# The normalised chunks of three norms: from three engines to VectorE alone, with the row of scales read in PSUM

## The chip, the cores and the metric

The kernel runs on one core of one Trainium2 chip. The metric is device time in microseconds (us). The engines of a core are named as in the profile: PE is TensorE (with PEld, its weight loads), DVE is VectorE, ACT is ScalarE, POOL is GpSimd and SP is SyncE, which here only issues DMAs.

## The reference, cut to what matters

Two transformer layers and one further block work on one sequence of 256 tokens and 1024 channels, all in float32. Each sub-layer begins with the same norm:

```
y = x * rsqrt(mean(x * x, over channels) + 1e-6) * g
h = y * (1 + scale) + shift            # layers 0 and 1; the last block has g alone
out = h @ W                            # the sub-layer's first projection
```

`scale` and `shift` come from a conditioning vector. Sub-layers: a linear recurrence, a routed feed-forward ("PEER": per token and head the 16 best of 128 x 128 experts, then all experts as two dense products with sparse weights), attention with forget gates, a second PEER, and then a block of three mixers and a gated feed-forward.

## The kernel before

**Layout.** Activations lie transposed: 8 chunks of 128 channels (partitions) by 256 tokens. The residual `x` is 8 chunks in SBUF. Every product is made three times in a reduced format (`mm3`): each operand is split in a high part and a low rest, so `out = wh*xh + wh*xl + wl*xh`. For an activation the parts are `hh` and `hl`; for a weight unit of 128 x 1024 they are `whi` and `wlo`.

**The weight stream.** All weights pass through one stream of units (class `Stream`): SP loads a unit (`raw`), ACT or DVE makes `whi`, DVE or POOL makes `wlo`. Which engine does it is fixed when the program is built, by a running estimate of each engine's load (`either`, `soonest`, class `Clock`). Four split units and three raw ones can be ahead of PE.

**The norm, twice.** A norm needs the sums of squares over all channels before it can scale, and PE would wait for that. So `early` starts the next projection on unnormalised input: `before_norm` splits `x*g` into `hh` and `hl`, PE multiplies four weight units (five in the last block) with them, and the per-token scale is applied to the product afterwards. Meanwhile the sums become `rstd` (a power on POOL), and PE spreads `rstd` over all partitions into a row of scales in PSUM: two products with the identity, written to columns 0 to 255 of `r`, a `ps2` tile of two banks (the name `ps<-ident,rstd` in the profile). ACT copies that row to SBUF as `rb`.

**After the early projections**, `after_early` (three of the five norms: the PEER of layer 0, the attention, the PEER of layer 1) does two things. It scales the four early products, `out(i)`: DVE multiplies the product in PSUM with `rb`, copies one column of it, and ACT adds that column as a bias. And it makes the true normalised chunks: chunk by chunk `x*gs*rb`, then `hh` on ACT and `hl` on DVE (`normed_split`). Of the eight chunks in the order `BANKS`, those at even places are made by DVE in one operation (`scalar_tensor_tensor`: x times a column times `rb`), those at odd places by ACT (x times the column, ahead of time) and POOL (times `rb`). PE needs `hh` and `hl`, in that order of chunks, for the next unit's product. In the last block the two norms don't come here: they use `rb` alone (`scaled`, and `unit` of the feed-forward).

**What orders the work.** A scheduler with its own timeline puts the instructions of each engine in an order when the program is built; each engine then runs its own list strictly in that order and waits on semaphores. The three places are called here the first (at about 198 us, PEER of layer 0), the second (1058 us, attention) and the third (1239 us, PEER of layer 1). In the PEERs `W` is scratch memory (the chunks and the queries lie there); at the second place the chunks lie in `raw_qk`. After `out(i)` the PEER multiplies the queries with the keys (`q_scores`, in the profile `pb<-W`), and that needs a PSUM bank which an early product held until `out(i)` had read it.

Of the kernel before, what the change touches and what calls it, by code (L numbers as in the profile page):

```python
# [11 lines left out]
AF = mybir.ActivationFunctionType  # L12
ALU = mybir.AluOpType
# [3 lines left out]
T = 256  # L17
# [299 lines left out]
class Kern:  # L317
# [100 lines left out]
    def early(self, x, gs, shift=None, how=None, count=4):  # L418


        nc, tc, hx, lx = self.nc, self.tc, self.hx, self.lx
        n = T
        if shift is not None:
            n = T + 2
            two = shift[:, 0:NCH, None].to_broadcast([P, NCH, 2])
            nc.scalar.copy(hx[:, :, T:], two)
            nc.vector.tensor_sub(lx[:, :, T:], two, hx[:, :, T:].bitcast(F32))
        outs = [self.ps() for _ in range(4)]
        outs += [o[:, T:] for o in outs[:count - 4]]
        r, b = self.ps2(), None  # L430
        w, step = {}, 0
        groups, rows_at, bcast_at = how or HOW
        groups += tuple((i,) for i in range(4, count))
        for g in groups:
            for i in g:
                w[i] = self.ws.get(i > 3)
            for k, c in enumerate(self.BANKS):
                s = slice(c * P, (c + 1) * P)
                for i in g:
                    with tc.issue_after(b.ins) if b is not None else nullcontext():  # L440
                        mm = self.mm3(outs[i][:, 0:n], *(t[:, s] for t in w[i]), hx[:, c, 0:n], lx[:, c, 0:n],
                                      k == 0, k == NCH - 1)
                    step += 1
                    if step == rows_at:
                        with tc.issue_after(mm.ins):
                            self.pow = r1 = self.rstd_rows(r[:, 512:])
                        for lo in los[1:2]:
                            with tc.issue_after(r1.ins):
                                lo(nc.gpsimd)
                        for lo in los[2:]:  # L450
                            lo(nc.vector)
                    if step == bcast_at:
                        with tc.issue_after(mm.ins):
                            b = self.rstd_bcast(r)
                        nc.scalar.copy(self.rb, r[:, 0:T])
            if g is groups[0]:
                with tc.issue_after(self.last_sq.ins):
                    los = self.ws.begin()
                for lo in los[:1]:
                    lo(nc.vector)  # L460
        self.normed = x, gs, shift
        return outs

    def scaled(self, outs, dst):
# [6 lines left out]
    def after_early(self, outs, dst, slots):  # L471

        nc = self.nc
        x, gs, shift = self.normed
        s = slots[0][:, 0:4]

        def out(i):
            nc.vector.tensor_mul(dst[i], outs[i][:, 0:T], self.rb)
            if shift is not None:
                nc.vector.tensor_copy(s[:, i:i + 1], outs[i][:, T:T + 1])  # L480
                nc.scalar.activation(dst[i], dst[i], AF.Identity, bias=s[:, i:i + 1])

        t = slots[1:]
        for c in self.BANKS[1::2]:
            nc.scalar.activation(t[c], x[:, c], AF.Copy, scale=gs[:, c:c + 1])
        few = len(outs) == 4
        for i in range(2 if few else 0):
            out(i)
        for k, c in enumerate(self.BANKS):
            if k % 2:  # L490
                h = nc.gpsimd.tensor_mul(t[c], t[c], self.rb)
            else:
                nc.vector.scalar_tensor_tensor(t[c], x[:, c], gs[:, c:c + 1], self.rb, op0=ALU.mult, op1=ALU.mult)
        for c in self.BANKS:
            h2 = self.normed_split(t[c], c, shift)
        self.h_there = h.ins, h2.ins
        for i in range(2 if few else 0, len(outs)):
            out(i)
        self.clock.level()
# [1489 lines left out]
```

## Time and profile before

| | us |
|---|---|
| median of 3 runs (2552.61, 2553.39, 2561.49) | 2553.39 |
| the profiled execution's own time | 2553.62 |
| its span | 2551.9 |
| PE busy in the span | 2455.8 (96%) |
| DVE busy | 1715.5 (67%) |
| ACT busy | 1249.5 (49%) |
| POOL busy | 1055.4 (41%) |

Between the span and the execution's own time lie 1.7 us. A timeline row reads: start, duration, engine, line, operation, out<-in with the names of the program, shape, how many instructions are merged in the row, and in brackets how long the engine was idle before it and who ended that. All work is recorded by one helper, so every row has line L225, and rows are told apart by tile names. PEclk is the TensorE clock that was granted, 1.00 for full speed. A row of the stage table gives, for a stretch of the span, the busy time of each engine, and PEclk.

### The profile page before, as it was taken

Reading aid. Unit: us, or ns where it says so; the run is one execution under the profiler, and the core shown is the slowest. Engines: PE = TensorE matmul, PEld = TensorE weight load, DVE = VectorE, ACT = ScalarE, POOL = GpSimd, SP = SyncE. Lnnn points to the kernel's source line nnn. Section 1 sums busy time; section 2 is a strip of 40 time slices with the busy share of each in tenths; the row PEclk is TensorE's granted clock in tenths of the full one; section 3 lists DMA queues with packets and bytes.
Section 4 is the critical chain, followed back from the end, with each engine's and each line's share of the span. In section 5 each row is a group of like instructions: output and inputs, shape, how many; then the busy total and the mean of one; then the engine's idle time right before and its main releaser. Section 6 shows DMA issues by size and latency. Waiting matters only on the chain.

```text
span 2551.9 us, 48864 instructions
## 1 busy us (share of the span) xinstructions
PE 2455.8 (96%) x19264; PEld 2390.3 (94%) x19264; DVE 1715.5 (67%) x3404; ACT 1249.5 (49%) x2031; POOL 1055.4 (41%) x654
## 2 busy tenths in 40 slices
PE   7879999999999999999999999999999999999998
PEld 7879999999999999878899999899999997999996
DVE  8798785765787755673787668465555558557764
ACT  4745555554444444544555555444444444444543
POOL 4477766779522100331577677870000015303310
PEclk9989999999999999998999999999999999999999
DMA  7855566678888865452556566885555554364654
GB/s 274 305 157 182 182 195 192 213 232 293 285 310 312 305 200 184 145 158 66 167 168 199 190 210 215 266 285 185 182 182 184 185 183 132 116 198 153 196 182 139
DMA packets 164134, 517.40 MB, mean 203 GB/s; under 512 B 18224, under 2 KB 51136, under 8 KB 162880
## 3 DMA queue, kind: packets, MB, share of 16 engines
q1 hardware_dynamic: 144720, 463.53, 55.7%
q0 software_dynamic: 8064, 29.36, 3.5%
q10 hardware_dynamic: 11120, 21.38, 2.4%
q8 instruction: 151, 2.47, 0.4%
q14 instruction: 79, 0.65, 0.1%
HBM read 484.85 MB, written 29.36 MB: 202 GB/s over the span
## 4 chain that ended last, share of the span: by engine, by line
PE 73%; DVE 8%; POOL 7%; issue 6%; DMA 4%; ACT 2%; SPq 0%; POOLq 0%; ACTq 0%; DVEq 0%
PE pb L225 38%; PE ps L225 35%; POOL W L225 5%; DVE mraw L225 2%; DVE wlo L225 1%; POOL wlo L225 1%; DVE hl L225 1%; DMA raw<-pv 1%; ACT whi L225 1%; DMA x<-gdram 1%; DVE W L225 0%; DVE tt L225 0%; DVE ri L225 0%; DMA mraw<-mod_ffn 0%; DMA raw<-pu 0%
## 5 line engine op out<-in xcount | busy, mean ns | idle before, releaser
L225 ACT CAST whi<-raw 128x1024 fp32r<-128x1024 f32 x741 | 777.1, 1050 | 945.9 <-PE ps L225 356.4
L225 DVE TENSOR_TENSOR wlo<-raw,whi 128x1024 fp32r<-128x1024 f32 x475 | 622.2, 1311 | 456.2 <-ACT whi L225 449.8
L225 POOL TENSOR_TENSOR wlo<-raw,whi 128x1024 fp32r<-128x1024 f32 x282 | 682.5, 2423 | 454.2 <-ACT whi L225 400.0
L225 PE MATMUL ps<-hh,whi 128*128 128x256 f32 x2736 | 780.6, 285 | 11.8 <-DVE W L225 5.5
L225 PE MATMUL ps<-hl,whi 128*128 128x256 f32 x2736 | 782.4, 286 | 6.7 <-DVE hl L225 6.7
L225 PE MATMUL ps<-hh,wlo 128*128 128x256 f32 x2736 | 777.9, 285 | 8.1 <-DVE wlo L225 5.0
L225 PE MATMUL pb<-hh,whi 128*128 128x256 f32 (+1 forms) x2512 | 715.4, 287 | 11.0 <-ACT whi L225 8.5
L225 PE MATMUL pb<-hl,whi 128*128 128x256 f32 (+1 forms) x2512 | 713.8, 285 | 3.6 <-DVE hl L225 3.4
L225 PE MATMUL pb<-hh,wlo 128*128 128x256 f32 (+1 forms) x2512 | 710.0, 284 | 4.3 <-POOL wlo L225 2.5
L225 PEld LDWEIGHTS ps<-hh,whi 128*128 128x128 f32 x2736 | 524.3, 192 | 13.5 <-DVE W L225 6.2
L225 PEld LDWEIGHTS ps<-hh,wlo 128*128 128x128 f32 x2736 | 525.2, 192 | 10.9 <-DVE wlo L225 6.9
L225 PEld LDWEIGHTS ps<-hl,whi 128*128 128x128 f32 x2736 | 522.6, 191 | 9.6 <-DVE hl L225 7.8
L225 PEld LDWEIGHTS pb<-hh,whi 128*128 128x128 f32 x2512 | 478.1, 191 | 12.8 <-ACT whi L225 9.5
L225 PEld LDWEIGHTS pb<-hh,wlo 128*128 128x128 f32 x2512 | 478.4, 191 | 6.0 <-POOL wlo L225 3.3
L225 PEld LDWEIGHTS pb<-hl,whi 128*128 128x128 f32 x2512 | 478.6, 191 | 4.5 <-DVE hl L225 4.5
L225 POOL TENSOR_TENSOR W<-W 128x256 f32<-128x256 f32 x12 | 9.3, 774 | 527.7 <-ACT W L225 527.7
L225 DVE SCALAR_TENSOR_TENSOR o<-pb,x 128x128 f32<-128x128 f32 (+1 forms) x512 | 196.4, 411 | 28.6 <-PE ps L225 27.5
L225 POOL TENSOR_TENSOR W<-W,x 128x384 f32<-128x384 f32 x128 | 180.1, 1446 | 4.4 <-DMA x<-gdram 2.7
L225 DVE TENSOR_TENSOR o<-pb,x 128x256 f32<-128x256 f32 (+1 forms) x256 | 106.8, 417 | 104.1 <-PE ps L225 72.8
L225 PE MATMUL ps<-o 128*128 128x128 f32 (+1 forms) x768 | 125.9, 276 | 0.0
L225 PEld LDWEIGHTS ps<-o 128*128 128x128 f32 x768 | 105.6, 190 | 0.0
L225 ACT COPY x<-ps 128x384 f32<-128x384 f32 x128 | 61.1, 477 | 55.4 <-PE ps L225 55.2
(400 smaller groups left out, 2891.4 us busy)
## 6 DMA issues: line engine op xcount, KB each, us to landing
raw<-pu SPq DMA_DIRECT2D x256, 512.0 KB, 3.8
raw<-pv SPq DMA_DIRECT2D x256, 512.0 KB, 4.3
x<-gdram SPq DMA_DIRECT2D x128, 192.0 KB, 4.0
raw<-w_rest SPq DMA_DIRECT2D x40, 512.0 KB, 3.8
raw<-pq SPq DMA_DIRECT2D x32, 512.0 KB, 4.0
mraw<-mod_mix SPq DMA_DIRECT2D x24, 512.0 KB, 6.0
gdram<-x ACTq DMA_DIRECT2D x64, 192.0 KB, 2.1
gdram<-x SPq DMA_DIRECT2D x64, 192.0 KB, 2.3
```

The lines of the kernel that those rows point to most:

```text
L225: return f(*args, **kw)
```

## The change

ACT no longer makes the four products x times column ahead of time, POOL no longer multiplies, and the copy of the row of scales to SBUF moves from ACT to DVE. DVE makes all eight chunks and reads the row of scales from `r` in PSUM; `rb` is still used for the early products. The copy moves at all five norms, the chunks at the three with `after_early`.

```diff
@@ in early
-                        nc.scalar.copy(self.rb, r[:, 0:T])
+                        nc.vector.tensor_copy(self.rb, r[:, 0:T])
...
-        self.normed = x, gs, shift
+        self.normed = x, gs, shift, r[:, 0:T]
@@ in after_early
-        x, gs, shift = self.normed
+        x, gs, shift, rp = self.normed
...
         t = slots[1:]
-        for c in self.BANKS[1::2]:
-            nc.scalar.activation(t[c], x[:, c], AF.Copy, scale=gs[:, c:c + 1])
         few = len(outs) == 4
         for i in range(2 if few else 0):
             out(i)
-        for k, c in enumerate(self.BANKS):
-            if k % 2:
-                h = nc.gpsimd.tensor_mul(t[c], t[c], self.rb)
-            else:
-                nc.vector.scalar_tensor_tensor(t[c], x[:, c], gs[:, c:c + 1], self.rb, op0=ALU.mult, op1=ALU.mult)
+        for c in self.BANKS:
+            h = nc.vector.scalar_tensor_tensor(t[c], x[:, c], gs[:, c:c + 1], rp, op0=ALU.mult, op1=ALU.mult)
         for c in self.BANKS:
             h2 = self.normed_split(t[c], c, shift)
```

The scheduler's order differs near the three places, by a single instruction at the copies in the last two norms, and in seven matmul rows ahead of the last norm; elsewhere each engine's list is the same, and every `whi` and `wlo` stays on its engine. Three pieces follow. Tiles are numbered in the order in which they are made, so the same tile has another number before and now.

DVE at the second place, from the first use of the row of scales; `raw_qk<-x,mod_mix` is a chunk, `z` and `og` are the scaled early products, `ps` is the row in PSUM. Before:

```order
L225 TENSOR_TENSOR z<-pb_12279,rb 128x256
L225 COPY raw_qk<-pb_12279 128x1
L225 TENSOR_TENSOR og<-pb_12280,rb 128x256
L225 COPY raw_qk<-pb_12280 128x1
L225 SCALAR_TENSOR_TENSOR raw_qk<-x,mod_mix,rb 128x256 x4
L225 TENSOR_TENSOR og<-pb_12281,rb 128x256
L225 COPY raw_qk<-pb_12281 128x1
L225 CAST whi<-raw 128x1024
L225 SCALAR_TENSOR_TENSOR hl<-raw_qk,mod_mix,hh 128x256 x2
L225 TENSOR_TENSOR og<-pb_12282,rb 128x256
```

Now:

```order
L225 COPY rb<-ps_12279 128x256
L225 SCALAR_TENSOR_TENSOR raw_qk<-x,mod_mix,ps_12279 128x256 x7
L225 TENSOR_TENSOR z<-pb_12275,rb 128x256
L225 COPY raw_qk<-pb_12275 128x1
L225 TENSOR_TENSOR og<-pb_12276,rb 128x256
L225 COPY raw_qk<-pb_12276 128x1
L225 SCALAR_TENSOR_TENSOR raw_qk<-x,mod_mix,ps_12279 128x256
L225 TENSOR_TENSOR og<-pb_12277,rb 128x256
L225 COPY raw_qk<-pb_12277 128x1
L225 CAST whi<-raw 128x1024
L225 SCALAR_TENSOR_TENSOR hl<-raw_qk,mod_mix,hh 128x256 x5
L225 TENSOR_TENSOR og<-pb_12278,rb 128x256
```

The copy and seven chunks now stand ahead of the first early product, and ahead of the first `hl` stand the same operations as before and, in addition, the copy and the four chunks that POOL made. The same holds at the first and the third place.

POOL at the second place; the first `wlo` is of a unit that the early projections use. Before:

```order
L225 TENSOR_TENSOR wlo_12312<-raw_12157,whi_12311 128x1024
L225 TENSOR_TENSOR raw_qk_12413<-raw_qk_12413,rb_101 128x256 x4
L225 TENSOR_TENSOR wlo_12498<-raw_12495,whi_12497 128x1024
L225 TENSOR_TENSOR wlo_12508<-raw_12501,whi_12507 128x1024
L225 TENSOR_TENSOR wlo_12564<-raw_12511,whi_12563 128x1024
```

Now:

```order
L225 TENSOR_TENSOR wlo_12308<-raw_12153,whi_12307 128x1024
L225 TENSOR_TENSOR wlo_12490<-raw_12487,whi_12489 128x1024
L225 TENSOR_TENSOR wlo_12500<-raw_12493,whi_12499 128x1024
L225 TENSOR_TENSOR wlo_12556<-raw_12503,whi_12555 128x1024
L225 TENSOR_TENSOR wlo_12615<-raw_12559,whi_12614 128x1024
```

The four products between the splits of two weight units are gone, so the second split no longer stands behind them. At the third place four products likewise stood behind `wlo_14092` and ahead of `wlo_14102` (now `wlo_14080` and `wlo_14090`).

PE at the third place, right after the early projections; `pb<-W` are the scores of the first three queries, `whi_13934` (now `whi_13926`) is the unit of the first projection on the true chunks. Before:

```order
L225 MATMUL pb3_14075<-W_14025 128x128 x2
L225 MATMUL pb0_14080<-W_14025 128x128 x2
L225 MATMUL pb1_14085<-W_14025 128x128 x2
L225 MATMUL pb3_14090<-hh_104,whi_13934 128x256
L225 MATMUL pb3_14090<-hl_105,whi_13934 128x256
L225 MATMUL pb3_14090<-hh_104,wlo_13935 128x256
```

Now, with the projection's next twelve matmuls left out:

```order
L225 MATMUL pb3_14063<-W_14017 128x128 x2
L225 MATMUL pb0_14068<-W_14017 128x128 x2
L225 MATMUL pb3_14078<-hh_104,whi_13926 128x256
...
L225 MATMUL pb1_14073<-W_14017 128x128 x2
L225 MATMUL pb3_14078<-hl_105,whi_13926 128x256
L225 MATMUL pb3_14078<-hh_104,wlo_13927 128x256
```

The third pair of scores, whose bank the last early product holds, moved from ahead of the projection to behind its thirteenth matmul.

## The prediction

> **What bounds the kernel now.** I read the page's header first, then the busy time by stage, cut at the three places of the change.
>
> ```profile
> span 2551.9 us, 48864 instructions
> core 0: us, PE busy (x) PEld busy (x) DVE busy (x) ACT busy (x) POOL busy (x), PEclk, DMA share, GB/s
> 199.00:215.00 16.00, 11.79 (x90) 10.79 (x89) 16.00 (x44) 8.79 (x23) 12.02 (x8) 1.00 0.50 186
> 215.00:571.00 356.00, 356.00 (x3009) 355.85 (x3009) 256.96 (x905) 193.66 (x377) 257.90 (x110) 1.00 0.64 202
> 1058.00:1076.00 18.00, 13.20 (x77) 11.70 (x77) 15.01 (x30) 10.35 (x23) 10.88 (x7) 0.81 0.50 161
> 1239.00:1258.00 19.00, 13.11 (x84) 12.39 (x83) 18.24 (x46) 8.29 (x22) 10.72 (x8) 0.73 0.41 148
> 1258.00:1604.00 346.00, 346.00 (x2925) 345.84 (x2924) 254.36 (x900) 189.10 (x369) 248.12 (x104) 1.00 0.62 196
> ```
>
> After the first and the third place PE is busy all the time for some 350 us, so a microsecond that PE gains at a place moves everything behind it. At the places themselves PE idles 16.00 - 11.79 = 4.2, 18.00 - 13.20 = 4.8 and 19.00 - 13.11 = 5.9 us: 14.9 us is the whole idle time that the change can reach. DVE is the busiest there. Which wait ends last is read from PE's timeline at the three places:
>
> ```profile
> 208.00 0.39 PE L225 MATMUL pb<-hl,whi 128*128 128x256 f32 x1 [1.44 <-DVE hl L225]
> 210.50 0.38 PE L225 MATMUL pb<-hl,whi 128*128 128x256 f32 x1 [1.33 <-DVE hl L225]
> ...
> 1066.72 0.58 PE L225 MATMUL ps<-hl,whi 128*128 128x256 f32 x1 [3.32 <-DVE hl L225]
> 1069.22 0.58 PE L225 MATMUL ps<-hl,whi 128*128 128x256 f32 x1 [1.48 <-DVE hl L225]
> ...
> 1245.90 0.84 PE L225 MATMUL pb<-W 128*128 128x128 f32 x4 [2.11 <-DVE pb L225]
> 1249.88 1.19 PE L225 MATMUL pb<-W 128*128 128x128 f32 x4 [3.14 <-DVE W L225]
> 1252.56 0.58 PE L225 MATMUL pb<-hl,whi 128*128 128x256 f32 x1 [0.63 <-DVE hl L225]
> ```
>
> Every long wait ends with DVE: an `hl`, or at the third place the early product whose bank the scores need. Why DVE is late stands in its timeline and POOL's at the same places (first, second, third):
>
> ```profile
> 205.43 2.52 DVE L225 SCALAR_TENSOR_TENSOR hl<-W,mod_ffn,hh 128x256 fp32r<-128x256 f32 x1
> 208.26 3.37 DVE L225 SCALAR_TENSOR_TENSOR hl<-W,mod_ffn,hh 128x256 fp32r<-128x256 f32 x4
> 205.12 5.04 POOL L225 TENSOR_TENSOR wlo<-raw,whi 128x1024 fp32r<-128x1024 f32 x2 [1.48 <-DVE whi L225]
> ...
> 1064.10 5.07 DVE L225 SCALAR_TENSOR_TENSOR hl<-raw_qk,mod_mix,hh 128x256 fp32r<-128x256 f32 x2
> 1069.48 2.06 DVE L225 SCALAR_TENSOR_TENSOR hl<-raw_qk,mod_mix,hh 128x256 fp32r<-128x256 f32 x5
> 1060.06 3.56 POOL L225 TENSOR_TENSOR raw_qk<-raw_qk,rb 128x256 f32<-128x256 f32 x4
> 1063.59 5.29 POOL L225 TENSOR_TENSOR wlo<-raw,whi 128x1024 fp32r<-128x1024 f32 x2
> ...
> 1245.76 2.98 DVE L225 SCALAR_TENSOR_TENSOR hl<-W,mod_ffn,hh 128x256 fp32r<-128x256 f32 x2
> 1249.66 3.64 DVE L225 SCALAR_TENSOR_TENSOR hl<-W,mod_ffn,hh 128x256 fp32r<-128x256 f32 x4
> 1245.71 2.35 POOL L225 TENSOR_TENSOR wlo<-raw,whi 128x1024 fp32r<-128x1024 f32 x1
> 1249.47 2.35 POOL L225 TENSOR_TENSOR wlo<-raw,whi 128x1024 fp32r<-128x1024 f32 x1 [1.41 <-issue]
> ```
>
> Five `hl` in a row take 2.06 us, 0.41 each, when POOL is idle. While POOL runs a `wlo`, one `hl` waits for that `wlo` to end: two of them take 5.07 us behind two `wlo` of 5.29. So a `wlo` that falls among the `hl` costs DVE about 2.1 us (5.07 less 2 x 0.41, halved), and PE behind it. There are two such `wlo` at each place.
>
> **The change part by part.** *The chunks.* What they cost now, and what a like operation costs that has one input in PSUM:
>
> ```profile
> L225 DVE SCALAR_TENSOR_TENSOR W<-x,mod_ffn,rb x8: 942/960/2105, 199.4 to 1244.2; 128x256 f32<-128x256 f32 x8
> L225 DVE TENSOR_TENSOR W<-pb,rb x8: 408/411/425, 198.6 to 1249.3; 128x256 f32<-128x256 f32 x8
> L225 ACT COPY rb<-ps x5: 347/373/373, 198.1 to 2361.0; 128x256 f32<-128x256 f32 x5
> 199.39 3.66 DVE L225 SCALAR_TENSOR_TENSOR W<-x,mod_ffn,rb 128x256 f32<-128x256 f32 x4
> 1059.75 3.28 DVE L225 SCALAR_TENSOR_TENSOR raw_qk<-x,mod_mix,rb 128x256 f32<-128x256 f32 x4
> 1240.44 4.72 DVE L225 SCALAR_TENSOR_TENSOR W<-x,mod_ffn,rb 128x256 f32<-128x256 f32 x4
> 1046.52 0.48 DVE L225 SCALAR_TENSOR_TENSOR x<-ps,mod_ffn,x 128x256 f32<-128x256 f32 x1
> 1046.91 0.57 DVE L225 SCALAR_TENSOR_TENSOR hl<-x,mod_mix,hh 128x256 fp32r<-128x256 f32 x1
> 1046.35 0.85 POOL L225 TENSOR_TENSOR W<-W 128x256 f32<-128x256 f32 x1 [142.82 <-ACT W L225]
> ```
>
> Four chunks from SBUF beside POOL's products take 3.28 to 4.72 us, about 0.95 each: each waits its turn with POOL. The eight early products, one input in PSUM, take 408 to 425 ns wherever they fall, and the `x<-ps` at 1046.52 takes 0.48 although POOL runs from 1046.35 to 1047.20; the next operation starts 0.39 after it. The new chunks have one input in SBUF and one in PSUM, like these. Their price lies between 0.39 (start to start) and 0.95 (no better than now); I take 0.39, since eight of eight nearest rows were not held up. So 8 x 0.39 = 3.1 us stands in place of 3.66, 3.28 and 4.72: a gain of 0.5, 0.2 and 1.6.
>
> [...]
>
> *The copy of the row.* ACT's copy took 0.37, and DVE waited for it. DVE's own lies between that and the 0.41 of an early product, less the 0.09 by which starts run ahead of ends: 0.33. At the first and second place it stands in place of the wait for ACT: nothing. At the third DVE was late itself and the copy adds 0.3. In the last two norms it adds at most 0.4 to DVE ahead of the early products; PE has the next unit's products queued there, and I put it at nothing (at worst 0.8 for both).
>
> *The products that go.* ACT's four and POOL's four (3.56 us) are not on PE's path in themselves. But POOL's stood ahead of a `wlo`, by order. At the second and third place that `wlo` can now start up to 3.5 us earlier, while DVE makes chunks with an input in PSUM and is not held up; only the `wlo` whose `whi` DVE itself makes, behind the chunks, is left among the `hl`. One block of 2.1 us less at each: 4.2. At the first place DVE makes the `whi` for the earlier of the two `wlo`, so both stay: nothing.
>
> *What this does to PE's clock.* Granted clock over the stretches where it was lowered:
>
> ```profile
> 1065.70:1072.10 6.40, 3.90 (x14) 3.43 (x15) 6.40 (x10) 2.85 (x8) 3.18 (x2) 0.50 0.49 165
> 1246.40:1256.50 10.10, 6.33 (x28) 5.76 (x28) 9.52 (x23) 3.21 (x12) 4.01 (x2) 0.50 0.29 104
> ```
>
> PE worked 3.90 and 6.33 us at half speed, half of it lost: 1.95 and 3.2. At the first place, with waits of 1.44 and 1.33, the clock stayed at 1.00. At the second place I expect waits of about 1.0 and 1.4 and no drop: 1.95 back. At the third a wait of about 2 us is left (the one `wlo`), in the part ahead of it the scores no longer hold PE, and half the loss comes back: between 0 and 3.2, I take 1.9. The moved scores themselves count nothing beyond that: the matmuls now ahead of them need the same `hl`. [...]
>
> *New waits.* At the second place ACT's list now has the `whi` of a unit ahead of seven `hh`, and that `whi` waits for a load:
>
> ```profile
> 1059.61 1.05 ACT L225 CAST whi<-raw 128x1024 fp32r<-128x1024 f32 x1 [0.69 <-DMA raw<-fox_qkv]
> ```
>
> So the first `hh` comes no earlier than 1060.7. DVE starts on its first `hl` only after the chunks, the three early products and a `whi`, near the 1064.10 of now, and PE runs out of early work at 1066.72 - 3.32 = 1063.4. The row's bank, where PE writes its next product but one, is free after the eighth chunk: the chunks now start at 1059.75, behind two early products, and with the same two ahead of the eighth it ends near 1059.75 + 3.1 = 1062.9. Both end in time: nothing, as long as the load is no later than now; each us that it is late beyond 1063 costs one.
>
> *The sum:* 0.5 + 0.2 + 1.6 - 0.3 + 4.2 + 1.95 + 1.9 = 10.05 us off the profiled execution's 2553.6 (1.7 us of it around the span): **2543.5**, 0.4% less. The median of the runs, 2553.4, is the same to 0.2.
>
> **The rivals.** *The blocks only move.* POOL's list is shorter, so a `wlo` may find another `hl` to hold up, two to a place as now, and the clock drops as now. Then only 0.5 + 0.2 + 1.3 = 2.0 is left: 2551.6. For it speaks the first place, where nothing frees POOL; against it, that each place has just two `wlo` in its neighbourhood and one of them has its `whi` ready before the chunks.
>
> *All stalls go.* With `hl` never held up, DVE keeps ahead of PE: 14.9 idle and 5.15 of clock come back, 2553.6 - 20 = 2533.6. Against it: one `wlo` still needs a `whi` from DVE in the middle of the `hl`.
>
> *Slower: the chunks are held up by POOL all the same.* If a second input in PSUM doesn't free them, each costs 0.95 and not 0.39: 24 x 0.56 = 13.4, the sum turns to 2553.6 - 10.05 + 13.4 = 2557. It decides from 0.39 + 10.05/24 = 0.81 us a chunk. For it speaks that all chunks beside POOL took 0.94 or more; against it the eight early products. [...]
>
> **How the numbers follow.** The forecast has a chance of 0.56 (its own range 2539 to 2548, from the clock and from a block more or less), the moved blocks 0.24, all stalls gone 0.12, slower 0.08. A measurement of this kernel can tell about 0.5%, 12.8 us, from no change, so faster means below 2540.6: all of the case without stalls and a quarter of the forecast, 0.12 + 0.14 = 0.26. Slower by 12.8 us needs chunks of 1.35 us, or something that I don't see: 0.03. Within: 0.71. The range of 2536 to 2553 leaves out the slower case and most of the case without stalls.
>
> **What would show it.** Right: chunks of 0.4 to 0.48 us in the DVE rows, whatever POOL does; a `wlo` on POOL during the chunks at the second and third place, and one stretched `hl` there instead of two; PEclk near 1.00 from 1058 to 1076; PE idle some 2 us less at each of these two. Wrong: chunks near 0.95; two stretched `hl`; an `hh` that waits for ACT at the second place; or a shift at the places that is gone again at the end of the span.

## The result and the profile after

| | before | after |
|---|---|---|
| median, shared runs | 2559.07 us (13 runs) | 2544.06 us (13 runs) |
| ratio of after to before, 95% interval | | 0.9946 [0.9932, 0.9961] |
| the same, in a second comparison | 2558.54 us (24 runs) | 2545.20 us (7 runs), 0.9948 [0.9930, 0.9966] |
| profiled execution, its span | 2553.62, 2551.9 us | 2542.43, 2540.7 us |

The changed kernel is 0.54% faster. The ratio leaves out one slow run of before (2630.93 us) and is estimated over the other runs, so it is not the quotient of the two medians. 2543.5 us had been forecast, and 2542.43 was profiled. The busy times of after:

```profile
PE 2447.5 (96%) x19264; PEld 2381.1 (94%) x19264; DVE 1718.4 (68%) x3421; ACT 1241.5 (49%) x2014; POOL 1044.3 (41%) x642
```

PE is busy 2447.5 us (before 2455.8) in a span that is 11.2 us shorter. Where it gained is seen in the busy time by stage at the three places, the rows that answer to those of before:

```profile
199.00:215.00 16.00, 12.31 (x98) 11.52 (x97) 15.90 (x47) 8.78 (x23) 9.67 (x4) 1.00 0.62 221
1057.00:1075.00 18.00, 16.97 (x101) 14.49 (x101) 16.52 (x42) 13.48 (x28) 6.98 (x3) 1.00 0.61 181
1233.00:1252.00 19.00, 16.32 (x134) 15.73 (x133) 17.57 (x69) 11.49 (x28) 12.05 (x5) 1.00 0.50 164
```

PE idles 16.00 - 12.31 = 3.7, 18.00 - 16.97 = 1.0 and 19.00 - 16.32 = 2.7 us (before 4.2, 4.8 and 5.9), and PEclk is 1.00 at all three (before 0.81 and 0.73 at the second and third). DVE, POOL and PE's waits in the timelines, place by place:

```profile
199.50 2.82 DVE L225 SCALAR_TENSOR_TENSOR W<-x,mod_ffn,ps 128x256 f32<-128x256 f32 x7
206.20 2.39 DVE L225 SCALAR_TENSOR_TENSOR hl<-W,mod_ffn,hh 128x256 fp32r<-128x256 f32 x1
208.91 2.98 DVE L225 SCALAR_TENSOR_TENSOR hl<-W,mod_ffn,hh 128x256 fp32r<-128x256 f32 x3
205.82 5.00 POOL L225 TENSOR_TENSOR wlo<-raw,whi 128x1024 fp32r<-128x1024 f32 x2 [4.52 <-DVE whi L225]
...
1057.86 2.82 DVE L225 SCALAR_TENSOR_TENSOR raw_qk<-x,mod_mix,ps 128x256 f32<-128x256 f32 x7
1062.78 4.21 DVE L225 SCALAR_TENSOR_TENSOR hl<-raw_qk,mod_mix,hh 128x256 fp32r<-128x256 f32 x5
1059.83 2.40 POOL L225 TENSOR_TENSOR wlo<-raw,whi 128x1024 fp32r<-128x1024 f32 x1 [0.77 <-ACT whi L225]
1062.99 2.52 POOL L225 TENSOR_TENSOR wlo<-raw,whi 128x1024 fp32r<-128x1024 f32 x1 [0.75 <-DVE whi L225]
...
1233.42 2.82 DVE L225 SCALAR_TENSOR_TENSOR W<-x,mod_ffn,ps 128x256 f32<-128x256 f32 x7
1240.65 2.99 DVE L225 SCALAR_TENSOR_TENSOR hl<-W,mod_ffn,hh 128x256 fp32r<-128x256 f32 x3
1233.30 4.76 POOL L225 TENSOR_TENSOR wlo<-raw,whi 128x1024 fp32r<-128x1024 f32 x2 [0.69 <-issue]
1240.07 2.50 POOL L225 TENSOR_TENSOR wlo<-raw,whi 128x1024 fp32r<-128x1024 f32 x1 [2.00 <-DVE whi L225]
```

Seven chunks take 2.82 us at every place, 0.39 from start to start, and at the second and third place POOL runs a `wlo` in the middle of them (1059.83, 1233.30): a chunk that reads the row from PSUM isn't held up there. At the first place two `hl` are still held up by two `wlo`, at the second and third only one: five `hl` in 4.21 are 5 x 0.41 = 2.05 and one block of 2.1.

```profile
205.19 1.16 PE L225 MATMUL pb<-W 128*128 128x128 f32 x8 [0.94 <-ACT W L225]
207.65 0.39 PE L225 MATMUL pb<-hh,whi 128*128 128x256 f32 x1 [1.29 <-ACT W L225]
211.16 0.38 PE L225 MATMUL pb<-hl,whi 128*128 128x256 f32 x1 [0.90 <-DVE hl L225]
...
1063.31 0.39 PE L225 MATMUL ps<-hl,whi 128*128 128x256 f32 x1 [0.52 <-DVE hl L225]
1065.85 0.38 PE L225 MATMUL ps<-hl,whi 128*128 128x256 f32 x1 [0.51 <-DVE hl L225]
...
1238.19 1.16 PE L225 MATMUL pb<-W 128*128 128x128 f32 x8 [1.38 <-ACT W L225]
1239.69 0.39 PE L225 MATMUL pb<-hh,whi 128*128 128x256 f32 x1 [0.35 <-ACT W L225]
1242.90 0.38 PE L225 MATMUL pb<-hl,whi 128*128 128x256 f32 x1 [0.96 <-DVE hl L225]
```

The waits of 3.32 and 3.14 are gone. New is a name: at the first and third place PE waits first for ACT (`W`: a query with its bias, then scores that ACT copies out of PSUM), and only then, for 0.9 to 1.0, for an `hl`.

**How the places are measured from here on.** Between the places the same work takes some us more or less from one execution to the next (the attention 129.0 in one profile and 135.0 in another; more on that at the end), so each place is measured by itself, from the start of the row of scales (`ps<-ident,rstd`) in PE's timeline to a matmul behind the place: at the first and third to the scores that follow 204 and 132 matmuls of the projections, at the second to the first transpose `pb<-ident,raw_qk`. (The first four expectations still took the second stretch up to the third place.) Where a kernel has its scores in another order at the third place, the next common one is taken, less the 3.31 us of each query between. Idle time is the length less PE's busy time over 30, 40 and 30 us from the row; the clock's loss is busy time x (1 - PEclk), summed over steps of 0.5 us. Four profiles of after and three of before, five of them from runs told below:

| | first | second | third | sum | PE idle | lost to the clock |
|---|---|---|---|---|---|---|
| before | 34.50 | 52.47 | 28.37 | 115.3 | 4.2 + 4.8 + 5.9 | 0 + 2.0 + 3.2 |
| before, b2 | 34.51 | 53.08 | 28.54 | 116.1 | 4.2 + 4.8 + 5.9 | 0 + 2.7 + 3.4 |
| before, b3 | 34.52 | 53.07 | 28.33 | 115.9 | 4.2 + 4.8 + 5.9 | 0 + 2.6 + 3.2 |
| after | 33.56 | 48.44 | 22.40 | 104.4 | 3.7 + 1.6 + 2.7 | 0 + 0 + 0 |
| after, c_after | 33.56 | 48.42 | 22.70 | 104.7 | 3.7 + 1.7 + 1.7 | 0 + 0 + 1.7 |
| after, a3 | 33.91 | 48.52 | 22.73 | 105.2 | 2.8 + 1.7 + 3.0 | 1.7 + 0 + 0 |
| after, a4 | 33.90 | 48.66 | 22.73 | 105.3 | 2.8 + 1.6 + 1.7 | 1.7 + 0 + 1.7 |

The means differ by 0.8, 4.4 and 5.8, together 10.9 us. That is the gain; the ratios, 10 to 17 and 9 to 18 us by their intervals, agree with it.

### The profile page after: what moved, and what is told of

It is laid out like the page before. It is cut to its first block, busy times and chain, and to the rows that moved or that the text cites. A ratio compares the mean times of both kernels' runs of the same rounds, so it can differ in the third digit from the quotient of the medians.

```text
span 2540.7 us, 48846 instructions
## 1 busy us (share of the span) xinstructions
PE 2447.5 (96%) x19264; PEld 2381.1 (94%) x19264; DVE 1718.4 (68%) x3421; ACT 1241.5 (49%) x2014; POOL 1044.3 (41%) x642
## 4 chain that ended last, share of the span: by engine, by line
PE 71%; DVE 8%; issue 6%; POOL 6%; DMA 6%; ACT 2%; SPq 0%; POOLq 0%; ACTq 0%; DVEq 0%
PE pb L225 37%; PE ps L225 34%; POOL W L225 4%; DVE mraw L225 2%; DMA raw<-pu 1%; DVE wlo L225 1%; DMA x<-gdram 1%; POOL wlo L225 1%; ACT whi L225 1%; DVE hl L225 1%; DMA raw<-pv 1%; DMA raw<-w_rest 1%; DMA x<-mod_mix 0%; DVE x L225 0%; DVE W L225 0%
## 5 line engine op out<-in xcount | busy, mean ns | idle before, releaser
L225 DVE TENSOR_TENSOR wlo<-raw,whi 128x1024 fp32r<-128x1024 f32 x475 | 630.9, 1329 | 447.7 <-ACT whi L225 443.0
L225 PE MATMUL ps<-hh,whi 128*128 128x256 f32 x2736 | 778.4, 285 | 12.6 <-DVE W L225 5.9
L225 PEld LDWEIGHTS ps<-hh,whi 128*128 128x128 f32 x2736 | 521.6, 191 | 14.9 <-DVE W L225 7.0
L225 DVE TENSOR_TENSOR o<-pb,x 128x256 f32<-128x256 f32 (+1 forms) x256 | 106.4, 416 | 104.4 <-PE ps L225 71.7
```

Source lines behind the costliest of these rows:

```text
L225: return f(*args, **kw)
```

## The experiments

The theory has three parts. (A) A chunk with the row in PSUM takes 0.39 us whatever POOL does. (B) POOL's products stood ahead of a `wlo`; without them it runs beside the chunks and not among the `hl`. (C) With the shorter waits PE's clock no longer falls. Rivals: the handover from ACT cost; or it doesn't matter where the row is read; or PE simply waited for POOL's half of the chunks. The kernels, with medians and places as above:

| kernel | median (runs) | ratio to before [95%] | first | second | third | sum | idle | clock |
|---|---|---|---|---|---|---|---|---|
| e1_copy | 2561.64 (10) | 1.000 [0.9983, 1.0017] | 36.42 | 53.82 | 28.23 | 118.5 | 15.6 | 8.0 |
| e2_sbuf | 2555.74 (10) | 0.9987 [0.9971, 1.0003] | 36.50 | 51.36 | 28.51 | 116.4 | 13.2 | 8.2 |
| e3_half | 2557.95 (10) | 0.9985 [0.9969, 1.0001] | 34.90 | 51.66 | 27.59 | 114.2 | 12.6 | 7.0 |
| e4_pool | 2548.70 (6) | 0.9958 [0.9930, 0.9985] | 34.02 | 49.93 | 24.47 | 108.4 | 9.9 | 1.6 |
| e5_actcopy | 2546.88 (6) | 0.9957 [0.9932, 0.9982] | 35.98 | 47.68 | 23.13 | 106.8 | 8.6 | 1.7 |
| e6_lo | 2546.26 (10) | 0.9957 [0.9935, 0.9979] | 33.92 | 47.50 | 25.10 | 106.5 | 6.2 | 5.0 |
| e7_lo_act | 2547.95 (10) | 0.9964 [0.9948, 0.9981] | 33.83 | 47.68 | 23.50 | 105.0 | 8.8 | 0.0 |

The first four ran beside before with 2558.91 us (27 runs), the last three beside before with 2558.54 and c_after with 2545.20.

### The copy alone

```diff
 # the kernel before
-nc.scalar.copy(self.rb, r[:, 0:T])
+nc.vector.tensor_copy(self.rb, r[:, 0:T])
```

> The kernel before with one part of the change alone: the copy of the row of scales is made by DVE; ACT and POOL still make their half of the chunks. Three stretches of the program are compared, each from the start of the row of scales (ps<-ident,rstd): the first to the scores of the merged queue (before 34.50 us, after 33.56), the second to the row of the third place (180.60, 175.09), the third to the seventh scores pb<-W (28.37, 22.40). My theory, the copy is worth next to nothing: 34.5, 180.6 and 28.4, each within 0.7, two stretched hl at each place as before, and a time within 2 us of the kernel before. Rival, the handover from ACT to DVE is what cost: the three stretches shorten by several us together, and the last two norms by some tenths each; 5 us or more off the time.

No gain, by the ratio: the handover from ACT is not what cost. The medians differ by 2.7 us the wrong way, which the interval allows for. The idle time is nearly that of before, 15.6 against 14.9. The third stretch came out as expected, the second too as it was defined there (180.4 up to the third place). The first missed, 36.42 for 34.5: 1.7 us of clock were lost there, where before lost none.

### Eight chunks on DVE, with the row read from SBUF

```diff
 # the changed kernel
-h = nc.vector.scalar_tensor_tensor(t[c], x[:, c], gs[:, c:c + 1], rp, ...)
+h = nc.vector.scalar_tensor_tensor(t[c], x[:, c], gs[:, c:c + 1], self.rb, ...)
```

> The changed kernel, but the eight chunks on DVE read the row of scales from the copy in SBUF, not from PSUM; ACT and POOL take no part. My theory, the place of that operand decides whether POOL holds a chunk up: a chunk takes 0.4 us while POOL is idle and waits for the whole wlo where POOL runs one. In the changed kernel a wlo ran beside the chunks at every place (197.99 to 201.30, 1059.83 to 1062.23, 1233.30 to 1238.06), so about 1.8, 2.1 and 2 to 4.2 us are lost there: stretches of 35.0 to 35.4, 177 to 179 and 24.5 to 27 us against 33.56, 175.09 and 22.40, and 5 to 10 us more than the changed kernel. Rival, that POOL's four products are gone is all that matters, and the operand's place nothing: the stretches of the changed kernel within 0.7 each, no stretched chunk.

Nearly the whole gain is gone. DVE's chunks and POOL's `wlo` beside them, first, second and third place of this kernel:

```profile
199.69 3.87 DVE L225 SCALAR_TENSOR_TENSOR W<-x,mod_ffn,rb 128x256 f32<-128x256 f32 x8
197.20 3.31 POOL L225 TENSOR_TENSOR wlo<-raw,whi 128x1024 fp32r<-128x1024 f32 x1
...
1064.98 5.50 DVE L225 SCALAR_TENSOR_TENSOR raw_qk<-x,mod_mix,rb 128x256 f32<-128x256 f32 x8
1065.97 2.64 POOL L225 TENSOR_TENSOR wlo<-raw,whi 128x1024 fp32r<-128x1024 f32 x1 [0.71 <-ACT whi L225]
...
1243.69 6.47 DVE L225 SCALAR_TENSOR_TENSOR W<-x,mod_ffn,rb 128x256 f32<-128x256 f32 x8
1242.59 4.92 POOL L225 TENSOR_TENSOR wlo<-raw,whi 128x1024 fp32r<-128x1024 f32 x2 [0.68 <-issue]
```

Eight chunks would take 8 x 0.39 + 0.08 = 3.2 us. They take 3.87 where POOL's `wlo` ends at 200.5, soon after they begin, 5.50 beside one `wlo` and 6.47 beside two. That is 0.7, 2.3 and 3.3 us of being held up, where 1.8, 2.1 and 2 to 4.2 were expected, and the rival, a stretch as in the changed kernel, is out at every place. The second stretch was as expected (178.0 up to the third place). The first and the third came out longer, 36.50 for 35.0 to 35.4 and 28.51 for 24.5 to 27: the clock fell there too, for 1.6 and 3.7 us, at the third place behind a wait of 4.4. The profile puts that wait down to ACT, but it ends with the early product whose copy (DVE, 1250.42) stands behind the eight held-up chunks (how that is told apart stands with the next kernel).

The edit also changed the order that the scheduler found: here two early products stand ahead of the chunks. So the changed kernel is not the cleanest comparison. e5_actcopy, told below, has this order at all three places but for the copy of the row and a move or two of a single instruction, and its chunks come from PSUM: they take 3.21 us at every place, and its places are 9.6 us shorter (106.8 against 116.4). With the clock (8.2 against 1.7) included, and as far as the copy counts for little, that is what the place of one operand is worth here.

### DVE's half from PSUM, ACT and POOL as before

```diff
 # the changed kernel
-for c in self.BANKS:
-    h = nc.vector.scalar_tensor_tensor(... rp ...)
+for c in self.BANKS[1::2]:
+    nc.scalar.activation(t[c], x[:, c], AF.Copy, scale=gs[:, c:c + 1])
+for k, c in enumerate(self.BANKS):
+    if k % 2:
+        h = nc.gpsimd.tensor_mul(t[c], t[c], self.rb)
+    else:
+        nc.vector.scalar_tensor_tensor(... rp ...)
```

> Half of the change: DVE copies the row and makes its four chunks from PSUM, but ACT and POOL still make the other four as before. My theory, the gain at the second and third place comes from POOL's products standing no longer ahead of a wlo: here they still stand there, so two stretched hl at each place again, and a clock below 1.00 at the second and third; only DVE's own four chunks get shorter (0.4 in place of 0.95 each). Stretches of about 34, 178 to 180 and 26 to 28 us; 2 to 5 us off the kernel before. Rival, the gain comes from the operand in PSUM alone, whoever makes the other four: stretches near 33.6, 175 and 22.4, and a time within 2 us of the changed kernel.

At the third place:

```profile
1230.19 1.64 DVE L225 SCALAR_TENSOR_TENSOR W<-x,mod_ffn,ps 128x256 f32<-128x256 f32 x4
1236.49 5.44 DVE L225 SCALAR_TENSOR_TENSOR hl<-W,mod_ffn,hh 128x256 fp32r<-128x256 f32 x4
1232.45 3.17 POOL L225 TENSOR_TENSOR W<-W,rb 128x256 f32<-128x256 f32 x4
1235.59 5.28 POOL L225 TENSOR_TENSOR wlo<-raw,whi 128x1024 fp32r<-128x1024 f32 x2
1236.43 0.14 DVE L225 COPY W<-pb 128x1 f32<-128x1 f32 x1
1236.72 1.19 PE L225 MATMUL pb<-W 128*128 128x128 f32 x4 [2.49 <-ACT hh L225]
```

DVE's four chunks take 1.64 us, 0.39 each, as (A) has it. But POOL's products stand ahead of two `wlo` again, these fall among the `hl`, and four `hl` take 5.44. The sum of the places is 1.2 to 2 us below that of before, of 10.9 that the whole change brings: (A) without (B) is worth little. The first place came out at 34.90, where about 34 was expected; 1.7 us of clock were lost there.

The last line seems to say that PE waits for ACT, and so for POOL's half of the chunks, as the rival has it. It doesn't. A matmul that waits for an early product's copy on DVE starts 0.145 to 0.148 us after that copy ends, in 18 such waits of eight profiles (1249.60 + 0.14 to 1249.88 in before), and one that waits for ACT's bias or copy starts 0.05 after. Here the copy ends at 1236.57 and the matmul starts at 1236.72, 0.15 later; the `hh` only happened to end in between. The wait of 1.23 at the first place is the same. So PE's long waits in this kernel end with DVE, and DVE is without a gap from its first chunk to its last `hl`, here and in before. The time agrees (0.9985), though the second stretch up to the third place, as it was expected, came out at 173.8 and not at 178 to 180; that stretch holds the attention, whose clock differs from run to run (0 to 8.5 us lost in seven profiles).

### POOL's products for nobody

```diff
 # the changed kernel; t[8] is memory that nothing reads
-for c in self.BANKS:
+for k, c in enumerate(self.BANKS):
     h = nc.vector.scalar_tensor_tensor(... rp ...)
+    if k % 2:
+        nc.gpsimd.tensor_mul(t[8], x[:, c], self.rb)
```

> The changed kernel, and POOL makes in addition four products of a chunk of x with the row in SBUF, into memory that nobody reads (at the first place ahead of the next wlo, at the second and third between the wlo). Nothing waits for them but POOL's own list. My theory, POOL's products cost only by the wlo that they push later, among the hl: at the second and third place one block of about 2.1 us returns, and with waits of 2 to 3 us PE's clock falls again: stretches of 33.6 to 35, 177 to 181 and 24 to 27 us, 4 to 9 us more than the changed kernel. Rival, POOL's products cost before because PE waited for their results (the chunks of odd place): here nobody waits for them, so the stretches stay at 33.56, 175.09 and 22.40 within 0.7.

Nobody waits for these products, and they cost 3.1 to 4 us of the 10.9 (places 108.4 against 104.4 to 105.3). DVE's and ACT's lists at the places are those of the changed kernel. The third place:

```profile
1240.77 0.75 POOL L225 TENSOR_TENSOR W<-x,rb 128x256 f32<-128x256 f32 x1
1241.46 2.37 POOL L225 TENSOR_TENSOR wlo<-raw,whi 128x1024 fp32r<-128x1024 f32 x1
1242.86 3.00 DVE L225 SCALAR_TENSOR_TENSOR hl<-W,mod_ffn,hh 128x256 fp32r<-128x256 f32 x3
1247.36 3.44 DVE L225 SCALAR_TENSOR_TENSOR hl<-W,mod_ffn,hh 128x256 fp32r<-128x256 f32 x3
```

A product of 0.75 us pushes the `wlo` from beside the chunks to 1241.46 to 1243.83, and the first of the next three `hl` waits for it: 3.00 for three, where the changed kernel takes 1.39. The second block is that of the changed kernel. At the second place the block that was expected did not return:

```profile
1061.65 2.40 POOL L225 TENSOR_TENSOR wlo<-raw,whi 128x1024 fp32r<-128x1024 f32 x1
1064.01 1.88 POOL L225 TENSOR_TENSOR raw_qk<-x,rb 128x256 f32<-128x256 f32 x2
1065.23 5.16 DVE L225 SCALAR_TENSOR_TENSOR hl<-raw_qk,mod_mix,hh 128x256 fp32r<-128x256 f32 x5
```

The pushed `wlo` ends at 1064.05, ahead of the first `hl`. There the products themselves hold DVE up: five `hl` take 5.16, where the changed kernel takes 4.21, the `whi` ahead of them 1.21 for 0.68, and PE waits 1.60 for 0.52. So POOL's products, with DVE and ACT as they are, make the second place some 1.4 us longer and the third 1.7 to 2.1. The clock fell at the third place alone (1.6), as it does in two profiles of the changed kernel too.

This is not all that (B) is about: only one of the four products stands ahead of the `wlo` that is pushed here, where in before all four do. In e3_half all four do again, two blocks fall among the `hl` at each place, and the places are another 5.7 us longer (2.7 of idle time and 5.4 of clock, which overlap). The rival, that PE waited for the results of these products, finds no support in e3_half, as told above.

The median of 2548.70 lies 3.5 to 4.6 us above those of the changed kernel, where 4 to 9 were expected; the intervals overlap.

### The copy back on ACT

```diff
 # the changed kernel
-nc.vector.tensor_copy(self.rb, r[:, 0:T])
+nc.scalar.copy(self.rb, r[:, 0:T])
```

> The changed kernel once more, beside the next three. If its gain at the three places is not chance, the stretches come out as in its first profile within 0.7 us each: 33.6 us at the first place (row of scales to the scores of the merged queue), 48.4 at the second (row of scales to the first transpose pb<-ident,raw_qk; before 52.5), 22.4 at the third, and the ratio to the kernel before lies between 0.993 and 0.997. If part of it was chance, above all the clock of the second and third place, one of them is 1.5 us or more longer.

> The changed kernel with one part undone: ACT makes the copy of the row of scales again; DVE still makes all chunks from PSUM. The chunks need the copy no longer, so DVE could start them 0.34 us earlier, and ACT's hh come 0.37 us later. My theory, the copy is worth next to nothing either way: each stretch within 0.5 us of 33.6, 48.4 and 22.4, the time within 1.5 us of the changed kernel. Rival, the copy on DVE costs (the kernel before with that copy alone came out 1 to 2 us longer at the first and second place): then 2 to 4 us less than the changed kernel.

The control came out as expected at all three places. With the copy on ACT the second place gained 0.7 to 1.0, the first lost 2.1 to 2.4 and the third 0.4 to 0.7, and neither side was right: beside the copy itself, the order that the scheduler finds with it has changed, and the first place shows it. Two early products stand ahead of the chunks again, and two `hl`, not three, ahead of the `whi` that starts POOL. The next three `hl` meet both `wlo` (DVE, then PE's second wait for them, first place):

```profile
204.34 5.48 DVE L225 SCALAR_TENSOR_TENSOR hl<-W,mod_ffn,hh 128x256 fp32r<-128x256 f32 x3
209.88 0.38 PE L225 MATMUL pb<-hl,whi 128*128 128x256 f32 x1 [1.87 <-DVE hl L225]
```

The wait of 1.87 is followed by a clock of 0.50 that takes 1.7 us. In time the two kernels are not told apart (0.9957 and 0.9948).

### The last `wlo` among the `hl` on DVE

```diff
 # class Stream, ahead; V is VectorE, G is GpSimd
-lo(self.k.lo_engine or self.k.either(1024))
+lo(self.k.lo_next.pop(0) if self.k.lo_next else self.k.lo_engine or self.k.either(1024))
 # at the end of after_early, place 0, 1, 2
+self.lo_next = list(((V, V), (G, V), (G, V))[self.place])
```

> The changed kernel, and the wlo that still fall among the hl go from POOL to DVE: the first two after the chunks at the first place, the second one at the second and third. DVE needs 1.2 us for a wlo and was held up for 2.1. At the first place they stand behind all hl in DVE's list, at the second behind seven of eight, at the third ahead of the first hl. My theory, the stretched hl are what is left of PE's waits: they go, 1 to 2.5 us at the first place, about 1.0 at the second (waits of 0.52 and 0.51) and 0 to 1 at the third; 2 to 4.5 us less than the changed kernel. Rival, the wait only changes its name, since PE then waits for ACT's queries, hh or for a wlo that comes later: stretches as in the changed kernel, within 0.7, or longer.

> The last two together: the wlo among the hl on DVE, and the copy of the row on ACT. My theory, as the kernel with the wlo on DVE, within 1.5 us. Rival, DVE is now the longest at the places and 0.34 us of copy at each comes back: 1 to 2 us less than that kernel.

The second place gained 0.9 to 1.2, as worked out. The first gained nothing: no `hl` is held up there any more, but PE's waits for ACT (0.93 and 1.29) are those of the changed kernel, and the clock fell behind them as it did in a3 and a4. The third lost 2.4 to 2.7, with a clock loss of 3.2 for 0 to 1.7:

```profile
1235.37 1.21 DVE L225 TENSOR_TENSOR wlo<-raw,whi 128x1024 fp32r<-128x1024 f32 x1
1236.50 3.37 DVE L225 SCALAR_TENSOR_TENSOR hl<-W,mod_ffn,hh 128x256 fp32r<-128x256 f32 x3
1236.77 2.42 POOL L225 TENSOR_TENSOR wlo<-raw,whi 128x1024 fp32r<-128x1024 f32 x1 [3.44 <-ACT whi L225]
```

DVE's own `wlo` stands ahead of the first `hl`, POOL is free for the unit after, and that `wlo` (1236.77) falls among the `hl` in the place of the one removed: three `hl` in 3.37. With the copy on ACT as well the first place shows the next limit:

```profile
210.16 2.35 DVE L225 TENSOR_TENSOR wlo<-raw,whi 128x1024 fp32r<-128x1024 f32 x2
218.57 1.04 ACT L225 CAST whi<-raw 128x1024 fp32r<-128x1024 f32 x1 [6.39 <-DMA raw<-pq]
219.94 0.71 PE L225 MATMUL pb<-W 128*128 128x128 f32 x4 [2.24 <-ACT W L225]
```

DVE makes the two `wlo` only at 210.16, the raw units that they read stay occupied until then, the load that follows lands at 218.57, and PE waits 2.24 us for a query behind that `whi` on ACT. The chain from the late `wlo` to the late load is argued from these rows, not tried apart. Against e6_lo the sum of the places is 1.5 us less, as the rival had it, and the median 1.7 us more: the two are not told apart. Neither kernel is faster than the changed one (0.9957 and 0.9964 against 0.9946 and 0.9948), so no version here beats it.

### The same two kernels again

> The kernel before once more, for a second profile of its three places. What the half clock takes at a place is counted as half of the PE work done at clock 0.50 there. My theory: the waits are the same in every run (idle time of 4.2, 4.8 and 5.9 us within 0.4), but whether the clock falls after them differs from run to run; in the first profile it did not fall at the first place by chance, and here or in the next run it does and takes about 1.7 us. Rival: what happens at a place follows from the waits alone: clock loss of 0.0, 2.0 and 3.2 us again within 0.3.

> The kernel before a third time. My theory: idle times of 4.2, 4.8 and 5.9 us within 0.4 each, clock losses that differ from those of the other two profiles by a step of about 1.7 us at one place or more. Rival: 0.0, 2.0 and 3.2 us of clock loss within 0.3.

> The changed kernel a third time. My theory: idle times of 3.7, 1.6 and 1.7 to 2.7 us, and the clock falls at no more than one of the three places, for about 1.7 us in all. Rival: its clock at the places is as often low as before, and the first two profiles were luck: 4 us or more of clock loss.

> The changed kernel a fourth time, with the same expectations: idle times of 3.7, 1.6 and 1.7 to 2.7 us, and at most about 1.7 us of clock loss in all. Rival: 4 us or more.

Each of the four is one execution: 2554.64 and 2553.27 us for before, 2552.59 (a3) and 2544.65 (a4) for after. Stage rows of after with a lowered clock, the first place in a3 and the third in c_after (PEclk is the third number from the end):

```profile
196.00:212.00 16.00, 13.20 (x94) 12.60 (x93) 15.91 (x47) 8.78 (x23) 9.68 (x5) 0.89 0.60 220
```

```profile
1231.70:1250.70 19.00, 17.29 (x131) 16.89 (x131) 17.59 (x69) 11.14 (x28) 12.07 (x5) 0.91 0.49 167
```

For before the rival was nearer: idle time to 0.1 and clock (0, 2.0 to 2.7, 3.2 to 3.4) are nearly the same in three profiles; only the second place lost 0.7 more in the last two than in the first, beyond the 0.3 that the rival allows. So the clock of 1.00 at the first place was no chance of the first profile. For after the clock fell at the first place in a3 (0.89), at the third in c_after (0.91) and at both in a4. My expectation of one fall at most held in a3 and not in a4 (two falls, 3.4 us), and the idle time at the first place was 2.8 in both, not 3.7. But the stretch hardly knows it: at the first place 0 us lost with 3.7 idle gives 33.56, 1.7 lost with 2.8 idle gives 33.91. While the clock is low PE is slower, DVE catches up, and the wait for the `hl` (0.90) that would follow is gone: in a3 PE is busy 4.00 of the 4.00 us from 206.00, at a clock of 0.71.

## Why the prediction was right, point by point

**The total.** 10.05 us were forecast, 10.9 were measured at the places (by place 0.8 for 0.5, 4.4 for 4.25, 5.8 for 5.3), and 2542.43 was profiled for 2543.5. That the profiled time came within 1.1 us is luck: another profile of the same program (a3) took 2552.59, with the places no more than 0.8 us longer. The ratio, 0.54%, lies just beyond the 0.5% at which faster was to begin, which had a chance of 0.26; the times themselves, 2542.43 and a median of 2544.06, stay above the 2540.6 that stood for it. The medians differ by 13 to 15 us, 2 to 4 more than the places. That difference shows in no profile: outside the places PE idles and loses as much in the four profiles of after as in the three of before, within their scatter. The intervals (10 to 17, 9 to 18) hold 10.9, so it need not be more than scatter; it stays open.

**The chunks: right.** 0.39 each from start to start. The group of the 16 chunks in the two PEERs (busy time, mean ns of one):

```profile
L225 DVE SCALAR_TENSOR_TENSOR W<-x,mod_ffn,ps 128x256 f32<-128x256 f32 x16 | 6.6, 472 | 0.0
```

A mean of 472 ns is no more than a single `hl` took with both inputs in SBUF and POOL idle (0.47 at 1069.31 and at 1243.64 in the same profile). The copy to SBUF did not pay here: e2_sbuf reads the copied row, and its places are 9.6 us longer than those of e5_actcopy and 11.5 longer than those of the changed kernel. What made the difference is where the row lies: beside POOL's `wlo`, eight chunks took 3.87 to 6.47 with both inputs in SBUF (e2_sbuf); with the row in PSUM seven took 2.82 beside a `wlo` (the changed kernel) and eight 3.21 (e5_actcopy).

**The copy of the row: right,** as far as the runs tell: alone it brought nothing (1.000), undone it was not told apart.

**The products and the blocks: right in place.** One block less at the second and third place, both left at the first. That the products were not on PE's path in themselves agrees with the traces: in before DVE has no gap from its first chunk to its last `hl`, and PE's long waits end with DVE. (The wait of 2.11, put down to `DVE pb` in its row, ends with an early product's copy too, 0.147 us after it, as was read.) The size of the term, 4.2, was not measured by itself. With one product ahead of a `wlo` e4_pool loses 3.1 to 4 of the 10.9, with all four, and half the chunks elsewhere, e3_half loses 9 to 10. The sum also took the chunks and the blocks as terms that add, and they don't: half the chunks from PSUM with the products left (e3_half) gain 1.2 to 2 us at the places, no products but chunks from SBUF (e2_sbuf) nothing (116.4 against 115.3 to 116.1), and both together 10.9.

**The clock: near in size, in part by luck.** 1.95 and 1.9 were expected; 2.4 and 2.4 came back in the mean of the profiles (2.0, 2.7, 2.6 before and none after at the second place; 3.2 to 3.4 before and 0, 1.7, 0, 1.7 after at the third). The half that was taken for the third place was an estimate that no run shows; it came out as three quarters (2.4 of 3.3). At the first place, where the sum had no term for it, the clock now falls in two of four profiles, for 1.7 each, and in before in none of three. So the net is 4.0 for 3.85. The waits alone do not decide it: in the same program, with waits equal to 0.01 us up to that point (1.38 and 0.35 in after, 1.37 and 0.34 in c_after), the clock falls in one execution and not in the other. What decides it no run shows.

**The new waits: the step that failed.** The `whi` that waits for its load cost nothing, as said. But ACT's own list at the first and third place was not costed, and so put at nothing. The first place of after:

```profile
201.83 2.91 ACT L225 ACTIVATE hh<-W,mod_ffn 128x256 fp32r<-128x256 f32 x7 [4.04 <-PE pb L225]
204.65 0.89 ACT L225 ACTIVATE W<-W 128x256 f32<-128x256 f32 x2
205.84 1.03 ACT L225 CAST whi<-raw 128x1024 fp32r<-128x1024 f32 x1
207.19 0.72 ACT L225 COPY W<-pb 128x128 f32<-128x128 f32 x4
```

The early products now stand behind seven chunks on DVE, and the scheduler put their biases behind seven `hh` on ACT (before, two biases came at 199.11, ahead of the `hh`). The products themselves are in time, the first two by 203.1, while PE has early work up to 205.19 - 0.94 = 204.25. What comes late are the biases, and behind a `whi` the copies of the scores: PE waits 0.94 + 1.29 us for ACT at the first place and 1.38 + 0.35 at the third. That is why the first place gained only 0.8, and why e6_lo could not gain there. At the third the forecast had a wait of about 2 us, for an `hl`; 1.7 of the 2.7 that are left are ACT's.

**The rivals.** Moved blocks: out at the second and third place. All stalls gone: out, 6 to 8 us of idle time are left. Slower by held-up chunks: out for this kernel; e2_sbuf has such chunks, and its places are 0.3 to 1.1 us longer than those of before, not 3.4 as was priced. A rival that was not listed is PE's moved scores at the third place. No run takes them alone, but e2_sbuf and e5_actcopy both have the third pair behind seven matmuls of the projection, and the place takes 28.51 us in one and 23.13 in the other.

## What to carry to other kernels

Here, where DVE works beside POOL, it mattered more where an operand lies than how many operations there are: it paid to read one of two inputs from PSUM and not to copy it to SBUF first (places of 104.4 to 105.3 us against 116.4 in e2_sbuf). Work on a third engine is not free because nobody waits for its result (e4_pool's products cost 3.1 to 4 us); look at what stands behind it in that engine's list. When a stall is taken away, look for the wait that it covered: here it was the bias on ACT (0.94 us), then a `wlo` of the next unit (three `hl` in 3.37), then a load (a wait of 2.24). And don't add up the gains of two parts where each covers the other: here either part alone brought 2 us or less, and both 10.9.

## What the runs showed of the hardware

PE's clock fell to 0.50 for 3.41 us or for two to four times as long: 6.83 us at the second place of before and 10.24 at the third (first profile), 3.4 at the third of c_after, 13.65 in the attention of before. A fall of 3.41 at a place lost 1.65 to 1.71 us; the two longer ones at the places of before, where PE idles in part, lost 2.0 and 3.2 in all. The same waits led to none or one such fall (the third place of after and of c_after). It also falls where PE has no wait at all. The stretch of attention between the second and third place, in after and then in c_after:

```profile
1096.80:1231.80 135.00, 135.00 (x840) 116.27 (x839) 77.13 (x140) 64.25 (x135) 30.05 (x19) 0.95 0.38 114
```

```profile
1101.60:1230.60 129.00, 129.00 (x841) 111.46 (x841) 77.14 (x140) 64.15 (x135) 30.10 (x19) 1.00 0.38 119
```

PE is busy all the time in both, the work is the same, and it takes 135.0 us with a clock of 0.95 and 129.0 with 1.00. Over all seven profiles of before and after the clock takes between 0 and 8.5 us there (8.5, 1.7, 1.7; 6.8, 0, 8.5, 1.7). This is as large as the effects studied, and it is why places were compared and not spans. Why it falls there no run shows.
